# A decoder trunk on one core: the rounded weights begin at eight different byte offsets in their buffers

## The chip, the cores and the metric

The kernel runs on one core of one Trainium2 chip. The metric is the time of one execution on the device, in microseconds (us). The engines are named as in the profile: PE is the matrix engine (its matmuls) and PEld its loads of weights, which overlap the matmuls; DVE is the vector engine, ACT the scalar engine, POOL the GpSimd engine, and SP issues most of the DMAs.

## The reference

The kernel computes a trunk of two layers on 512 tokens of width 1024, in float32. Layer 0 mixes tokens with a gated delta rule, layer 1 with attention over a window of 128 tokens that reads one shared projection of keys and values. After each mixer comes a gated channel mixer with a short convolution.

```python
for layer in range(DEPTH):                       # DEPTH = 2
    if layer < N_A_LAYERS:                       # layer 0
        h = h + gated_deltanet(rmsnorm(h, a_norm_w[i]), a_w_in[i], ..., a_w_out[i])
    else:                                        # layer 1
        k_sh, v_sh = shared_kv(h, kv_norm_w, w_kv)
        h = h + sliding_window_sink_attention(rmsnorm(h, b_norm_w[j]), k_sh, v_sh, b_w_q[j], ...)
    h = h + conv_gated_mlp(rmsnorm(h, ffn_norm_w[layer]), ffn_w_up[layer], ..., ffn_w_down[layer])
return rmsnorm(h, final_norm_w)
```

Nearly all of its arithmetic is in products with weight matrices: `a_w_in` (1024 by 6176), `a_w_out` (2048 by 1024), `w_kv`, `b_w_q`, `b_w_o`, and for each layer `ffn_w_up` (1024 by 5632) and `ffn_w_down` (2816 by 1024).

## The kernel before, in words

Activations lie transposed, with features on the 128 partitions and the 512 tokens along a row, so a matmul has a 128 by 128 block of a weight matrix as its stationary operand and 512 tokens (or half of them, 256) as its moving one. To keep the accuracy of float32 at the speed of the rounded type `float32r`, every operand is split into a rounded part and the rest: `whi` and `wlo` for weights, `xh` and `xl` for activations. A product is three matmuls, `whi*xh`, `whi*xl` and `wlo*xh` (`mm3`, L165, L166, L167). In the down projections and in a part of the output projection, a scheme of seven half products in place of eight is used, with 256 tokens to a matmul (`product`, L1049, L1050, L1051); the attention's query and output projections use `one_by_one` (L1336, L1338, L1340).

A weight block comes from memory by a DMA of 1 MB into a tile `stage` (two buffers; every third one in the down projections into `st3`). Then a **casting** makes the two parts: `cast` (L131) and, for a tile filled in two pieces, `weights` with `cast_to` (L152, L155). ACT copies the block into `whi` with rounding (L135 or L158) and DVE subtracts that from the block into `wlo` (L136 or L159). Each of `whi` and `wlo` has three buffers of 4096 bytes per partition, eight blocks of 128 columns one after the other, so block `k` of a buffer begins 512 bytes after block `k-1`, and one load of weights reads 512 consecutive bytes in each partition. There are 288 castings in the program: 49 for the input projections, then those of the output projection, of layer 0's channel mixer, of the attention and of layer 1's channel mixer.

All large tiles of the kernel begin at multiples of 512 bytes; the tiles `gap_x` and `gap_w`, to which nothing is written, fill up what small constants leave. The three buffers of `whi` lie at 204288, 208384 and 212480, those of `wlo` at 216576, 220672 and 224768, and `stage` at 187904 and 196096. Constants such as `ident` and `identr` (the unit matrix, plain and rounded) lie at odd places, both at 288 bytes past a multiple of 512.

The order of the instructions in the first part comes from a table of numbers (`ORDER`), later from the order in the code with priorities, and in the attention PE's order is written out by hand.

Of the kernel before, what the change touches and what calls it, by code (L numbers as in the profile page):

```python
# [9 lines left out]
F32R = mybir.dt.float32r  # L10
# [7 lines left out]
P = 128  # L18
# [26 lines left out]
def kernel(  # L45
# [37 lines left out]
    def nm(s):  # L83
        cnt[0] += 1
        return f"{s}_{cnt[0]}"

    wpool = ctx.enter_context(tc.tile_pool(name="weights", bufs=1, side="right"))
# [41 lines left out]
        return w[r0 : r0 + kt * P, c0 : c0 + 256].rearrange("(k p) c -> p k c", p=P)  # L129

    def cast(st, kt, half, m=P):  # L131
        hi = wpool.tile([P, 8, P], F32R, tag="whi", bufs=3, name=nm("whi"))
        lo = wpool.tile([P, 8, P], F32R, tag="wlo", bufs=3, name=nm("wlo"))
        src = st[:, :kt, half * P : half * P + m]
        S.copy(hi[:, :kt, :m], src)  # L135
        V.tensor_tensor(lo[:, :kt, :m], src, hi[:, :kt, :m].bitcast(F32), op=ALU.subtract)  # L136
        return hi, lo
# [8 lines left out]
    def cast_rows(rows, half):  # L146
        w = weights()
        for i, r in enumerate(rows):
            cast_to(w, 2 * i, r[:, :, half * P : half * P + P])
        return w  # L150

    def weights():  # L152
        return [wpool.tile([P, 8, P], F32R, tag=t, bufs=3, name=nm(t)) for t in ("whi", "wlo")]

    def cast_to(w, at, src):  # L155
        n = src.shape[1]
# [135 lines left out]
    def project(c0, i):  # L292
        if c0 not in held_stage:
            held_stage[c0] = load_stage(win, 0, 8, c0)
        ps = bank("d")
        passes[c0 + P * i] = mm3(ps[:], cast(held_stage[c0], 8, i), KD, xh, xl)
        return ps
# [14 lines left out]
    S.dma_start(gst[:, :, 0:16], win[:, c_b : c_b + 16].rearrange("(k p) c -> p k c", p=P))  # L312
    S.dma_start(gst[:, :, 32:48], win[:, c_b + 16 : c_b + 32].rearrange("(k p) c -> p k c", p=P))
    gw = cast(gst, KD, 0, m=48)
    gps = bank("d")
    mm3(gps[:48, :], gw, KD, xh, xl, m=48)
# [62 lines left out]
    def hc(ap):  # L379
# [45 lines left out]
        tag="f",  # L425
# [351 lines left out]
    for pos, word in enumerate(" ".join(ORDER).split(), 1):  # L777
        name, _, later = word.partition("@")
# [117 lines left out]
    def ffn(l, h, last=False):  # L896
# [22 lines left out]
        for t0, t1 in ((0, 12), (12, NF)):  # L919
# [3 lines left out]
            for t in range(t0, t1, 2):  # L923
                if l == 0 and t == 6:
                    bias_rows()
                sg = load_stage(wup, 0, 8, t * P)
                sv = load_stage(wup, 0, 8, DFF + t * P)
                f = []
                for j in range(2):
                    a = up(cast(sg, 8, j), t + j, "ga")  # L930
                    S.activation(a[:], a[:], AF.Silu)  # L931
                    b = up(cast(sv, 8, j), NF + t + j, "va")
                    V.tensor_tensor(b[:], a[:], b[:], op=ALU.mult)  # L933
                    f.append(b)
                sevens.append(forms(*f, rows, plain))
# [122 lines left out]
    def seven_products(sts, srcs, parts, sevens, hp, odd):  # L1058
# [3 lines left out]
        for u in range(2):  # L1062
# [19 lines left out]
            yield  # L1082
        e = bank("p" if odd else "g")[:, 0:256]
        w4 = weights()
        for u in range(2):
            w = cast(sts[u], 2 * len(parts[u]), 0)
# [16 lines left out]
    def seven_products_late(sts, parts, sevens, hp):  # L1103
# [11 lines left out]
        add(h11, a)  # L1115
        add(h11, b)
        ws, w4 = [], weights()
        for u in range(2):
            ws.append(cast(sts[u], 2 * len(parts[u]), 0))
# [453 lines left out]
```

## Time and profile before

| what | value |
|---|---|
| median of 2 runs | 1395.07 us (1393.67 to 1396.46) |
| the profiled execution | 1399.02 us |
| its span, first to last instruction | 1396.9 us |
| granted PE clock over the span | 0.996 |
| instructions | 22206 |
| DMA | 154.97 MB, mean 111 GB/s |

The profile page gives each engine's busy time in the span, the chain of waits that ended last, and groups of equal instructions by line with their count and mean time. The trace behind it can be asked for one line, for a stretch of time, or for a timeline. A matmul's end in it is modelled and the next one begins before it, so the pace of PE is read from where successive matmuls begin, not from how long one lasts.

### The profile page before, as it was taken

Reading aid. Unit: us, or ns where it says so; the run is one execution under the profiler, and the core shown is the slowest. Engines: PE = TensorE matmul, PEld = TensorE weight load, DVE = VectorE, ACT = ScalarE, POOL = GpSimd, SP = SyncE. Lnnn points to the kernel's source line nnn. Section 1 sums busy time; section 2 is a strip of 40 time slices with the busy share of each in tenths; the row PEclk is TensorE's granted clock in tenths of the full one; section 3 lists DMA queues with packets and bytes.
Section 4 is the critical chain, followed back from the end, with each engine's and each line's share of the span. In section 5 each row is a group of like instructions: output and inputs, shape, how many; then the busy total and the mean of one; then the engine's idle time right before and its main releaser. Section 6 shows DMA issues by size and latency. Waiting matters only on the chain.

```text
span 1396.9 us, 22206 instructions
## 1 busy us (share of the span) xinstructions
PE 1374.1 (98%) x8520; PEld 1171.4 (84%) x8520; DVE 1142.2 (82%) x2152; ACT 765.0 (55%) x1483; POOL 15.1 (1%) x33
## 2 busy tenths in 40 slices
PE   7999999999999999999999999999999999999998
PEld 5788888878887998889988889877788889988897
DVE  5896896978867987889958899788658889878996
ACT  7765575757558455544434446677545444444443
POOL 1000000000100000000000000000000000000000
PEclk9999999999999999999999999999999999999999
DMA  5334154162567432321343224312122221432222
GB/s 162 97 100 144 46 168 142 61 197 91 172 204 241 135 132 92 120 68 66 111 151 121 74 85 135 121 59 74 61 91 91 91 94 63 145 103 81 96 76 76
DMA packets 164029, 154.97 MB, mean 111 GB/s; under 512 B 24340, under 2 KB 150869, under 8 KB 163925
## 3 DMA queue, kind: packets, MB, share of 16 engines
q1 hardware_dynamic: 161522, 153.11, 34.2%
q8 instruction: 67, 1.10, 0.3%
q10 hardware_dynamic: 2403, 0.46, 0.2%
q14 instruction: 37, 0.30, 0.1%
HBM read 136.74 MB, written 15.75 MB: 109 GB/s over the span
## 4 chain that ended last, share of the span: by engine, by line
PE 91%; DVE 3%; DMA 2%; ACT 2%; issue 1%; ACTq 0%; DVEq 0%; SPq 0%
PE d L165 20%; PE d L167 19%; PE d L166 19%; PE g L201 2%; PE d L1051 2%; PE d L1049 2%; PE d L1050 2%; PE s L1050 1%; PE s L1049 1%; PE s L1051 1%; PE d L1336 1%; PE d L1340 1%; PE d L1338 1%; PE g L1050 1%; PE g L1051 1%; PE g L1049 1%
## 5 line engine op out<-in xcount | busy, mean ns | idle before, releaser
L165 PE MATMUL d<-xh,whi 128*128 128x512 f32 x1128 | 443.9, 396 | 1.5 <-ACT whi L135 1.3
L167 PE MATMUL d<-xh,wlo 128*128 128x512 f32 x1128 | 443.3, 395 | 0.5 <-DVE wlo L136 0.5
L166 PE MATMUL d<-xl,whi 128*128 128x512 f32 x1128 | 442.3, 394 | 0.0
L135 ACT CAST whi<-stage 128x1024 fp32r<-128x1024 f32 (+2 forms) x238 | 231.5, 977 | 227.4 <-PE d L166 131.5
L136 DVE TENSOR_TENSOR wlo<-stage,whi 128x1024 fp32r<-128x1024 f32 (+2 forms) x238 | 268.6, 1131 | 54.7 <-ACT whi L135 53.0
L165 PEld LDWEIGHTS d<-xh,whi 128*128 128x128 f32 x1128 | 212.2, 188 | 46.2 <-ACT whi L135 1.8
L167 PEld LDWEIGHTS d<-xh,wlo 128*128 128x128 f32 x1128 | 212.0, 188 | 44.5 <-DVE wlo L136 1.2
L166 PEld LDWEIGHTS d<-xl,whi 128*128 128x128 f32 x1128 | 212.2, 188 | 42.9
L283 DVE SCALAR_TENSOR_TENSOR acc<-d,cwc,acc 128x511 f32<-128x511 f32 (+2 forms) x96 | 70.2, 737 | 5.6 <-ACT acc L280 4.8
L909 DVE TENSOR_TENSOR sz<-d,p6s 128x512 f32<-128x512 f32 x58 | 40.0, 689 | 39.3 <-PE d L167 37.2
L931 ACT ACTIVATE dt<-dt 128x512 f32<-128x512 f32 x44 | 27.8, 632 | 80.8 <-DVE dt L914 80.8
L914 DVE SCALAR_TENSOR_TENSOR va<-sz,fcw,va 128x511 f32<-128x511 f32 (+1 forms) x58 | 43.4, 748 | 2.1 <-ACT va L912 1.2
L914 DVE SCALAR_TENSOR_TENSOR dt<-sz,fcw,dt 128x511 f32<-128x511 f32 (+1 forms) x58 | 43.4, 747 | 1.7 <-ACT dt L912 0.9
L564 DVE TENSOR_TENSOR sT<-sT,p6s 64x31 f32<-64x31 f32 (+15 forms) x124 | 40.8, 329 | 1.6
L558 DVE TENSOR_TENSOR p6s<-sN,sT 64x31 f32<-64x31 f32 (+15 forms) x124 | 40.6, 327 | 1.5
L1405 ACT ACTIVATE dt<-dt,sm 128x256 f32<-128x256 f32 (+1 forms) x64 | 30.1, 471 | 21.5 <-DVE sm L1388 21.5
L135 ACT CAST whi<-st 128x768 fp32r<-128x768 f32 (+1 forms) x30 | 23.8, 792 | 31.3 <-PE g L1050 8.5
L909 DVE TENSOR_TENSOR zl<-d,p6s 128x512 f32<-128x512 f32 x30 | 20.7, 688 | 22.7 <-PE d L167 22.7
L693 ACT ACTIVATE rq<-o 128x128 f32<-128x128 f32 x64 | 19.0, 297 | 35.7 <-DVE o L688 26.2
L933 DVE TENSOR_TENSOR va<-dt,va 128x512 f32<-128x512 f32 x44 | 30.4, 691 | 1.2
L136 DVE TENSOR_TENSOR wlo<-st,whi 128x768 fp32r<-128x768 f32 (+1 forms) x30 | 27.0, 902 | 2.1 <-ACT whi L135 1.7
L912 ACT ACTIVATE dt<-sz,normc,fcw 128x512 f32<-128x512 f32 x29 | 23.6, 814 | 7.1 <-DVE sz L909 6.9
(865 smaller groups left out, 2973.6 us busy)
## 6 DMA issues: line engine op xcount, KB each, us to landing
stage<-in_ffn_w_up_dram SPq DMA_DIRECT2D x44, 1024.0 KB, 4.9
stage<-in_a_w_in_dram SPq DMA_DIRECT2D x23, 1024.0 KB, 5.5
stage<-in_ffn_w_down_dram SPq DMA_DIRECT2D x16, 768.0 KB, 4.9
stage<-in_a_w_out_dram SPq DMA_DIRECT2D x8, 1024.0 KB, 6.3
st<-in_ffn_w_down_dram SPq DMA_DIRECT2D x8, 768.0 KB, 5.3
zd<-sz SPq DMA_DIRECT2D x16, 256.0 KB, 2.0
od<-o SPq DMA_DIRECT2D x16, 256.0 KB, 2.4
stage<-in_b_w_q_dram SPq DMA_DIRECT2D x4, 1024.0 KB
```

Of the source, the lines that this page charges most:

```text
L135: S.copy(hi[:, :kt, :m], src)
L136: V.tensor_tensor(lo[:, :kt, :m], src, hi[:, :kt, :m].bitcast(F32), op=ALU.subtract)
L165: PE.matmul(ps, hi[:, k, :m], xh[k], start=first and k == 0, stop=False)
L166: PE.matmul(ps, hi[:, k, :m], xl[k][:], start=False, stop=False)
L167: done.append(PE.matmul(ps, lo[:, k, :m], xh[k], start=False, stop=last and k == kt - 1))
L283: V.scalar_tensor_tensor(acc[:, d:], ps[:, : T - d], col, acc[:, d:], op0=ALU.mult, op1=ALU.add)
L564: V.tensor_tensor(Tm[:, s + 1 : 32, 0:m], Tm[:, s + 1 : 32, 0:m], tv, op=ALU.subtract)
L909: V.tensor_tensor(u[:], ps[:], rs[:], op=ALU.mult)
L914: V.scalar_tensor_tensor(acc[:, d:], u[:, : T - d], tap(2 - d, t), acc[:, d:], op0=ALU.mult, op1=ALU.add)
L1049: PE.matmul(ps, w[0][:, wk, :], hi, start=first and k == 0, stop=False, **kw)
L1050: PE.matmul(ps, w[0][:, wk, :], lo, start=False, stop=False, **kw)
L1051: PE.matmul(ps, w[1][:, wk, :], hi, start=False, stop=k == n - 1, **kw)
```

## The change

`cast` now takes its two tiles from `weights`. `weights` allocates buffers of 4608 bytes in place of 4096, counts its calls, and returns a view of 4096 bytes that begins `d` elements of 4 bytes into the buffer. Up to the 84th call `d` is 0. After that it is taken from `PLACES`, each entry for fourteen calls: 16 bytes for calls 85 to 97, 256 bytes for 98 to 111, then 0, 64, 128, 192, 32, 96, 16, 256, 0, 64, 128, 192, and 32 bytes for calls 280 to 288. The 85th call is in the up projection of layer 0's channel mixer.

```diff
     def cast(st, kt, half, m=P):
-        hi = wpool.tile([P, 8, P], F32R, tag="whi", bufs=3, name=nm("whi"))
-        lo = wpool.tile([P, 8, P], F32R, tag="wlo", bufs=3, name=nm("wlo"))
+        hi, lo = weights()
         src = st[:, :kt, half * P : half * P + m]
...
+    PLACES = [0, 16, 32, 48, 8, 24, 4, 64]
+    rounded = [0]
+
     def weights():
-        return [wpool.tile([P, 8, P], F32R, tag=t, bufs=3, name=nm(t)) for t in ("whi", "wlo")]
+        flat = [wpool.tile([P, 9 * P], F32R, tag=t, bufs=3, name=nm(t)) for t in ("whi", "wlo")]
+        rounded[0] += 1
+        d = PLACES[rounded[0] // 14 % 8] if rounded[0] > 84 else 0
+        return [t[:, d : d + 8 * P].rearrange("p (k c) -> p k c", k=8) for t in flat]
```

The larger buffers move their neighbours: `whi` now lies at 201216, 205824 and 210432, `wlo` at 215040, 219648 and 224256, and `stage` at 184832 and 193024, all of them multiples of 512 still. No other tile moves. On each of the five engines the instructions, their operands' shapes, their order and their waits are the same as before, row for row; only addresses differ.

## The prediction

> **What bounds the kernel now.** I read the page's first part (how busy each engine is), then the chain of waits, and then a table by stretches of time, since only addresses change and the question is which engine could feel an address.
>
> ```profile
> PE 1374.1 (98%) x8520; PEld 1171.4 (84%) x8520; DVE 1142.2 (82%) x2152; ACT 765.0 (55%) x1483; POOL 15.1 (1%) x33
> ...
> PE 91%; DVE 3%; DMA 2%; ACT 2%; issue 1%; ACTq 0%; DVEq 0%; SPq 0%
> PE d L165 20%; PE d L167 19%; PE d L166 19%; PE g L201 2%; PE d L1051 2%; PE d L1049 2%; PE d L1050 2%; PE s L1050 1%; PE s L1049 1%; PE s L1051 1%; PE d L1336 1%; PE d L1340 1%; PE d L1338 1%; PE g L1050 1%; PE g L1051 1%; PE g L1049 1%
> ```
>
> PE is the bound: it makes up 91% of the chain, and the lines that carry it are the products with rounded weights. So the time depends on the step from one such matmul to the next. The timeline shows that step, for 512 tokens and for 256 (columns: start in us, modelled length, engine and line, operands):
>
> ```profile
> 1100.12 0.39 PE L167 MATMUL d<-xh,wlo 128*128 128x512 f32 x1
> 1100.35 0.39 PE L165 MATMUL d<-xh,whi 128*128 128x512 f32 x1
> 1100.57 0.39 PE L166 MATMUL d<-xl,whi 128*128 128x512 f32 x1
> 1100.80 0.39 PE L167 MATMUL d<-xh,wlo 128*128 128x512 f32 x1
> ...
> 1190.30 0.28 PE L1049 MATMUL s<-f,whi 128*128 128x256 f32 x1
> 1190.42 0.28 PE L1050 MATMUL s<-f,whi 128*128 128x256 f32 x1
> 1190.54 0.28 PE L1051 MATMUL s<-f,wlo 128*128 128x256 f32 x1
> ```
>
> The wide step is 0.68/3, or 0.227 us; the narrow one is 0.12 us. The stretches give the same with what else is busy. Their bounds are those of the change's groups of fourteen castings: 585 to 649 us is where calls 85 to 97 are used (16 bytes), and so on (columns: stretch, its length, then PE, PEld, DVE, ACT and POOL with busy us and count, PE clock, DMA share, GB/s):
>
> ```profile
> core 0: us, PE busy (x) PEld busy (x) DVE busy (x) ACT busy (x) POOL busy (x), PEclk, DMA share, GB/s
> 585.00:649.00 64.00, 64.00 (x296) 53.49 (x295) 54.04 (x81) 30.61 (x42) 0.00 (x0) 1.00 0.26 86
> 649.00:680.00 31.00, 30.96 (x257) 30.62 (x255) 29.70 (x54) 14.02 (x21) 0.00 (x0) 1.00 0.32 103
> ...
> 721.00:797.00 76.00, 76.00 (x337) 62.93 (x336) 62.85 (x89) 35.32 (x49) 0.00 (x0) 1.00 0.28 95
> ...
> 839.00:864.00 25.00, 25.00 (x209) 24.85 (x208) 24.48 (x48) 14.07 (x24) 0.00 (x0) 1.00 0.36 117
> ...
> 949.00:1052.00 103.00, 102.79 (x646) 82.82 (x646) 71.67 (x184) 59.16 (x138) 0.00 (x0) 1.00 0.20 66
> 1052.00:1128.00 76.00, 76.00 (x337) 62.93 (x336) 63.70 (x93) 36.85 (x51) 0.00 (x0) 1.00 0.30 97
> ...
> 1335.00:1361.00 26.00, 24.99 (x207) 24.61 (x206) 24.89 (x50) 12.02 (x21) 0.00 (x0) 1.00 0.31 102
> ```
>
> PE is busy through all of these. DVE, the next engine, has room in the wide stretches (62.85 of 76 us) and next to none in three narrow ones: 29.70 of 31, 24.48 of 25 and 24.89 of 26 us.
>
> **The change, part by part.** No instruction is added, removed or moved, no DMA, no wait. Three things read or write at new addresses: PE's loads of weights, ACT's rounding copy, DVE's subtraction.
>
> First the counts. Of 204 castings after the 84th, 28 fall on place 0 and keep their offset. Counted in the changed code, the other places carry these matmuls, wide and narrow: 16 bytes 600 and 36; 32 bytes 270 and 186; 96 bytes 336 and none; 64 bytes 528 and 108; 128 bytes 384 and 189; 192 bytes none and 420; 256 bytes 144 and 396. I part them in two: 16, 32 and 96 are no multiples of 64 (1206 wide, 222 narrow, 1428 in all), the rest are (1056 wide, 1113 narrow). Together 3597 matmuls.
>
> *Loads.* The trace of before already loads weights from other places than multiples of 512:
>
> ```profile
> L165 PEld LDWEIGHTS d<-xh,whi 128*128 128x128 f32 x1120 | 211.3, 189 | 45.4 <-ACT whi L135 1.8 <-issue 0.6 <-ACT xh L175 0.5
> L468 PEld LDWEIGHTS g<-mnegr,identr x16: 187/188/192, 51.0 to 317.9; 128*128 128x128 f32 x16
> L594 PEld LDWEIGHTS s<-Xg,nt x128: 101/108/108, 129.0 to 386.8; 32*32 32x32 f32 x128
> L602 PEld LDWEIGHTS s<-sy,pz x128: 101/108/108, 136.6 to 393.4; 32*32 32x32 f32 x128
> L1432 PEld LDWEIGHTS p<-acc,Vp x152: 132/137/137, 916.9 to 998.8; 128*64 128x64 f32 x152
> ```
>
> `identr` of L468 has the same shape and type as `whi` and begins 288 bytes past a multiple of 512, so 32 past one of 64; its load has a median of 188 ns, as L165's has a mean of 189. L602 loads from steps of 128 bytes, L594 always from 128 past: 101/108/108 ns both. L1432's `Vp` blocks begin at 0 and 256: 132 to 137 ns. The load's length thus shows no price of the place.
>
> Whether the next matmul is late is a second question, and the timeline around L468 answers it nearly:
>
> ```profile
> 50.76 0.39 PE L165 MATMUL d<-xh,whi 128*128 128x512 f32 x1
> 50.99 0.39 PE L467 MATMUL g<-gr,skr 128*128 128x512 f32 x1
> 51.22 0.40 PE L468 MATMUL g<-mnegr,identr 128*128 128x512 f32 x1
> 51.45 0.39 PE L166 MATMUL d<-xl,whi 128*128 128x512 f32 x1
> 51.68 0.40 PE L467 MATMUL g<-gr,skr 128*128 128x512 f32 x1
> 51.92 0.39 PE L468 MATMUL g<-mnegr,identr 128*128 128x512 f32 x1
> 52.15 0.40 PE L167 MATMUL d<-xh,wlo 128*128 128x512 f32 x1
> 52.38 0.39 PE L165 MATMUL d<-xh,whi 128*128 128x512 f32 x1
> 52.61 0.40 PE L166 MATMUL d<-xl,whi 128*128 128x512 f32 x1
> 52.85 0.50 PE L467 MATMUL g<-gr,skr 128*128 128x512 f32 x1
> ```
>
> From 50.76 to 52.85 are nine steps in 2.09 us, 232 ns each, 5 over the plain 227. But L167 to L165 to L166 here, with buffers at multiples of 512, take 230 each as well, so the 5 ns belong to this busy place and not to `identr`. As the upper end I still charge 5 ns to every matmul off a multiple of 64: 1428 by 5 is 7.1 us. The lower end is nothing, unless the present step holds a cost that a new place removes; that is a rival below. I take 1 us, close to nothing, because the row nearest in kind, L468's load, shows no difference at the trace's step of 1 ns.
>
> By the Trainium skill ("SBUF — State Buffer", Specifications) the buffer memory has lines of 16 bytes, with a price for each new line. All eight places are multiples of 16, so by that rule a load would touch 32 lines wherever it begins and the sum would be 0; were the line 64 bytes, places 16, 32 and 96 would touch nine lines in place of eight. No run so far shows the line.
>
> *Castings.* Here too before has unaligned neighbours:
>
> ```profile
> L914 DVE SCALAR_TENSOR_TENSOR dt<-sz,fcw,dt 128x511 f32<-128x511 f32 x29 | 21.6, 746 | 0.9 <-ACT dt L912 0.9
> L176 DVE SCALAR_TENSOR_TENSOR xl<-h,normc,xh 128x512 fp32r<-128x512 f32 x16 | 11.3, 749 | 0.0
> L220 ACT CAST identr<-ident x1: 281/281/281, 8.8 to 8.8; 128x128 fp32r<-128x128 f32 x1
> L135 ACT CAST whi<-stage 128x1024 fp32r<-128x1024 f32 x174 | 181.8, 1050 | 156.1 <-PE d L166 117.0 <-DMA stage<-in_ffn_w_up_dram 11.0 <-PE d L1338 7.9
> L135 ACT CAST whi<-stage 128x512 fp32r<-128x512 f32 x17 | 10.4, 618 | 13.9 <-PE p L1050 4.4 <-DMA stage<-in_ffn_w_down_dram 3.3 <-DVE wlo L136 3.2
> L136 DVE TENSOR_TENSOR wlo<-stage,whi 128x1024 fp32r<-128x1024 f32 x174 | 212.1, 1221 | 50.4 <-ACT whi L135 49.1 <-ACT rt L869 0.7 <-PE s L662 0.2
> ```
>
> L914 reads and writes `dt` from 4 bytes in: 746 ns, against 749 for L176 that begins at multiples of 512 with one element more. ACT's copy into `identr`, 288 past, took 281 ns for 128 columns; from the two rows of L135, 432 ns for 512 columns, a copy of 128 at a multiple of 512 would take 618 - 384 x 0.844, or 294. So neither is slower off its place. Were they, most of it would be hidden: ACT idles 156.1 us ahead of L135 because the buffer is not free yet, and DVE has 13 us of room in 76. Only the three tight stretches have none. How long DVE works there on instructions that read `whi` or write `wlo`, the stretches' sum for that tile tells:
>
> ```profile
> sum 82.00, DVE 36.37; mean DVE 12.12
> ```
>
> 25% on these 36.37 us, far over what L914 allows, would be 9.1 us, less the 2.9 us of room in those stretches (1.3 + 0.52 + 1.11): 6 us as the upper end, and 0 as the value taken, from L914.
>
> *Base addresses.* The buffers move by multiples of 512. Before, the eight blocks of each buffer already begin at eight successive multiples of 512, and the step is 227 or 120 ns through all of them (rows above). Nothing is charged. `stage` moves by 3072 bytes and its DMAs keep their shape: nothing.
>
> The sum is +1 us against the profiled execution of 1399.02 us, which is 0.3% over the median of 1395.07. Against the median it gives 1396.
>
> **The rivals.**
>
> *Slower: a load that begins off a multiple of 64 is no longer hidden under a matmul.* For it: the load lasts 188 ns of a step of 227, so 39 ns more would show, and in the narrow steps loads overlap each other already. If it lasted half as long again, 94 ns, a wide step would become 282 ns, 55 more by 1206, and a narrow one up to 94 more by 222: 66 + 21 = 87 us, or 1482. It passes 2% (27.9 us) from 19.5 ns per matmul on these 1428; if every place but 0 paid, from 7.8 ns on 3597. Against it: L468's load at 188 ns. Its weak side is that no row begins at 16 past, where 636 of the matmuls are.
>
> *Slower: DVE becomes the bound.* To lose 27.9 us in the three tight stretches alone, their 36.37 us of subtractions would have to grow by 85%, to cover 27.9 and the room of 2.9. L914 speaks against any such growth.
>
> *Faster: the step itself holds a conflict.* Wide minus narrow is 107 ns for 256 columns, so 512 columns take 214 and 13 ns per matmul are something else. If these came of operands that begin alike, and new places removed them, 3597 by 13 is 46.8 us: 1348. Against it: the step is the same for eight blocks at different addresses, and L468 with both operands elsewhere is no faster. The Trainium skill ("TensorE: Matmul & The Clock Gate", Back-to-back issue gap) gives N/2.4 + 2.5 ns, 216 for 512 columns, an estimate that leaves 11 ns of this step open and would give some 40 us to such a conflict, about 1355; the trace does not agree with that pace here, and nothing in it says that the place is why.
>
> *The change doesn't reach what its words say.* It starts at the 85th casting, at 585 us, well after the output projection. That shortens what it can touch to the last 803 us, and is in the counts above.
>
> **How the numbers follow.** No difference to speak of: 0.81. Loads that stick out, or DVE: 0.14 for over 2% (0.10 and 0.04). A conflict removed: 0.05 for over 2%. Two per cent is about what a measurement of this kernel can tell from no change. The likeliest time is 1396. The range takes the upper ends of loads and castings, 7.1 + 6, on 1395, and a milder form of the first rival (another 5 ns per matmul, 7.1): 1415. Downward, a sixth of the conflict's 46.8 us: 1387.
>
> **What would show it.** Two stretches have equal work, fourteen castings and 336 wide matmuls: one at place 64 (721 to 797 us before), one at place 16 (1052 to 1128). They should again take 76 us each. Loads of `whi` should stay at 188 ns, L135 at 1050 and L136 at 1221 ns for 1024 columns. If the second stretch is longer than the first, the place of the load or of the casting counts, and the timeline's step (227 or more) says which. A step under 227 in the groups off 0 would make the third rival right; DVE near 100% where it had 82% the second.

## The result, and the profile after

| | before | after |
|---|---|---|
| median, us | 1395.07 (1393.67 to 1396.46, 2 runs) | 1404.34 (1403.34 to 1405.33, 2 runs) |
| ratio to before, 95% interval | | 1.0059 (1.0042 to 1.0076) |
| span of the profiled execution, us | 1396.9 | 1403.2 |

The changed kernel is 0.6% slower: inside the range, clear of noise, and nine times the 1 us that the sum gave. Its profile page shows the same picture as before, PE as the bound:

```profile
PE 1379.5 (98%) x8520; PEld 1168.8 (83%) x8520; DVE 1142.8 (81%) x2152; ACT 764.4 (54%) x1483; POOL 15.1 (1%) x33
...
PE 90%; DVE 3%; DMA 3%; ACT 2%; issue 1%; SPq 0%; DVEq 0%; ACTq 0%
```

DVE and ACT are busy as long as before (1142.2 and 765.0 us then); PE is busy 5.4 us longer for the same 8520 matmuls. The stretches by group of fourteen castings show where. The columns are those of the same view of before; the rows are, in order, place 16 for the first time, place 64, place 16 for the second time, place 256 with wide matmuls, and a narrow stretch at place 0 and, for some of its matmuls, 256:

```profile
585.00:644.00 59.00, 59.00 (x262) 48.87 (x261) 49.70 (x73) 26.62 (x36) 0.00 (x0) 1.00 0.25 82
718.10:796.50 78.40, 78.40 (x337) 63.26 (x337) 63.01 (x89) 35.58 (x48) 0.00 (x0) 1.00 0.26 87
...
1054.60:1133.00 78.40, 78.40 (x337) 63.54 (x336) 65.21 (x94) 37.07 (x51) 0.00 (x0) 1.00 0.30 96
1133.10:1165.00 31.90, 31.90 (x142) 26.41 (x141) 27.23 (x41) 13.95 (x20) 0.00 (x0) 1.00 0.23 77
1180.00:1211.00 31.00, 31.00 (x260) 31.00 (x260) 28.47 (x50) 12.30 (x17) 0.00 (x0) 1.00 0.48 157
```

The two stretches of equal work, 76 us each before, both take 78.4 now, with the same 337 matmuls, while DVE has over 13 us of room. The timeline inside the stretch at place 64 gives the step (L170 to L172 are L165 to L167 of before), and the rows after the dots are narrow ones at place 64:

```profile
749.64 0.39 PE L170 MATMUL d<-xh,whi 128*128 128x512 f32 x1
749.87 0.40 PE L171 MATMUL d<-xl,whi 128*128 128x512 f32 x1
750.11 0.39 PE L172 MATMUL d<-xh,wlo 128*128 128x512 f32 x1
750.34 0.40 PE L170 MATMUL d<-xh,whi 128*128 128x512 f32 x1
...
1213.91 0.28 PE L1054 MATMUL s<-qT,whi 128*128 128x256 f32 x1
1214.03 0.28 PE L1055 MATMUL s<-qT,whi 128*128 128x256 f32 x1
1214.14 0.28 PE L1056 MATMUL s<-qT,wlo 128*128 128x256 f32 x1
1214.26 0.28 PE L1054 MATMUL s<-sy,whi 128*128 128x256 f32 x1
1214.38 0.28 PE L1055 MATMUL s<-sy,whi 128*128 128x256 f32 x1
1214.49 0.28 PE L1056 MATMUL s<-sy,wlo 128*128 128x256 f32 x1
1214.61 0.28 PE L1054 MATMUL d<-vt,whi 128*128 128x256 f32 x1
```

A wide step is 0.70/3, 0.233 us, where it was 0.227; a narrow one 0.70/6, 0.117, where it was 0.120. So the wide steps became longer and the narrow ones shorter at this place. Over the whole trace, the means of all steps from one matmul with rounded weights to the next (those over 300 ns, which hold waits, left out; "first" and "second" are the two groups of castings at place 16):

| place, bytes | 0 | 16, first | 16, second | 32 | 64 | 96 | 128 | 192 | 256 |
|---|---|---|---|---|---|---|---|---|---|
| wide step, ns | 228 | 226.7 | 233.3 | 233 | 233.3 | 234 | 232.4 | none | 226.8 |
| matmuls | 1452 | 264 | 336 | 242 | 528 | 310 | 384 | | 144 |

The 228 of place 0 is a mean over two things. In an unbroken stretch the step there is 226.7 ns; but the first steps after other work on PE, up to ten of them, take some 231 ns, and the early part of the program is full of such breaks.

What did not change are the lengths of the castings and of the loads beside the wide matmuls, in the groups by line (L134 and L135 cast, L170 loads):

```profile
L134 ACT CAST whi<-stage 128x1024 fp32r<-128x1024 f32 x174 | 181.5, 1048 | 162.8 <-PE d L171 119.6 <-DMA stage<-in_ffn_w_up_dram 10.6 <-PE d L1343 8.3
L135 DVE TENSOR_TENSOR wlo<-stage,whi 128x1024 fp32r<-128x1024 f32 x174 | 212.0, 1221 | 47.1 <-ACT whi L134 43.5 <-DMA Xg<-td 2.2 <-ACT rt L874 0.7
L170 PEld LDWEIGHTS d<-xh,whi 128*128 128x128 f32 x1120 | 210.8, 188 | 47.2 <-ACT whi L134 1.4 <-ACT xh L180 0.7 <-issue 0.6
```

### The profile page after: what moved, and what is told of

Read it like the earlier page. It is cut to its first block, busy times and chain, and to the rows that moved or that the text cites. A ratio compares the mean times of both kernels' runs of the same rounds, so it can differ in the third digit from the quotient of the medians.

```text
span 1403.2 us, 22206 instructions
## 1 busy us (share of the span) xinstructions
PE 1379.5 (98%) x8520; PEld 1168.8 (83%) x8520; DVE 1142.8 (81%) x2152; ACT 764.4 (54%) x1483; POOL 15.1 (1%) x33
## 4 chain that ended last, share of the span: by engine, by line
PE 90%; DVE 3%; DMA 3%; ACT 2%; issue 1%; SPq 0%; DVEq 0%; ACTq 0%
PE d L170 19%; PE d L172 19%; PE d L171 19%; PE d L1056 2%; PE d L1054 2%; PE g L206 2%; PE d L1055 2%; PE s L1055 1%; PE s L1054 1%; PE s L1056 1%; PE d L1341 1%; PE d L1345 1%; PE d L1343 1%; PE g L1056 1%; PE g L1055 1%; PE g L1054 1%
## 5 line engine op out<-in xcount | busy, mean ns | idle before, releaser
L170 PE MATMUL d<-xh,whi 128*128 128x512 f32 x1128 | 445.8, 397 | 1.4 <-ACT whi L134 0.9
L172 PE MATMUL d<-xh,wlo 128*128 128x512 f32 x1128 | 445.2, 396 | 0.5 <-DVE wlo L135 0.5
L134 ACT CAST whi<-stage 128x1024 fp32r<-128x1024 f32 (+2 forms) x238 | 231.2, 975 | 234.3 <-PE d L171 134.8
L135 DVE TENSOR_TENSOR wlo<-stage,whi 128x1024 fp32r<-128x1024 f32 (+2 forms) x238 | 268.2, 1129 | 51.1 <-ACT whi L134 47.2
L170 PEld LDWEIGHTS d<-xh,whi 128*128 128x128 f32 x1128 | 211.8, 188 | 48.0 <-ACT whi L134 1.4
L172 PEld LDWEIGHTS d<-xh,wlo 128*128 128x128 f32 x1128 | 212.2, 188 | 47.0 <-DVE wlo L135 1.2
L134 ACT CAST whi<-st 128x768 fp32r<-128x768 f32 (+1 forms) x30 | 23.8, 792 | 31.7 <-PE g L1055 7.9
L135 DVE TENSOR_TENSOR wlo<-st,whi 128x768 fp32r<-128x768 f32 (+1 forms) x30 | 26.9, 900 | 1.8 <-ACT whi L134 1.4
```

Source lines behind the costliest of these rows:

```text
L170: PE.matmul(ps, hi[:, k, :m], xh[k], start=first and k == 0, stop=False)
L172: done.append(PE.matmul(ps, lo[:, k, :m], xh[k], start=False, stop=last and k == kt - 1))
```

## The experiments

The first question was whether the place does it at all, or the moved buffers. Theory P: the place in the buffer sets PE's step. The ratios below are against the kernel before, run on the same chip.

**All castings at place 0, with the larger buffers.**

```diff
-        d = PLACES[rounded[0] // 14 % 8] if rounded[0] > 84 else 0
+        d = 0
```

> The larger buffers and the moved base addresses stay, but every casting begins at place 0. Theory P (the place within 512 bytes sets the step of the matmuls): steps of 227 and 120 ns throughout, time as before, 1395 us. Rival B (the moved bases of whi, wlo and stage cost the time): about 1404 us, and slower somewhere at place 0.

Measured: 1395.45 us, ratio 0.9995 (0.9985 to 1.0006); mean steps 227.6 and 120.7 ns, against 227.6 and 120.6 before. The larger buffers and the new base addresses cost nothing that shows.

**All castings at place 64.** The line becomes `d = 16` (16 elements of 4 bytes).

> Every casting, the first 84 too, begins 64 bytes in. Theory P: all 3990 wide matmuls step at 233.3 ns instead of 226.7, +26 us, and all 2139 narrow ones at 118 instead of 120, -4 to -5 us: about 1417 us. Rival T (the longer steps belong to the later part of the program, not to the place): the first 585 us stay as they were, about 1404 us or less.

Measured: 1413.20 us, ratio 1.0120 (1.0104 to 1.0137). Every wide stretch, the first one from 13.8 us on too, steps at 233.4 ns in the mean; the narrow step has a mean of 116.6. The place does it, anywhere in the program. The gain in the narrow steps was larger than expected in ns: they take one of two paces, 117.8 ns in some stretches and 113.3 in others.

**All castings at place 192,** the one that no wide matmul of the changed kernel had: `d = 48`.

> Every casting begins 192 bytes in; no wide matmul of the changed kernel had this place. Theory F (every place that is no multiple of 256 makes the wide step 233 ns): about 1413 us, like place 64. Rival Q (each place has a step of its own, whole slots of 6.7 ns beside the 213.3 ns of 512 columns; at 192 the wide step may be 220 or 227): 227 ns would give about 1394 us, 220 ns about 1370 us. Narrow steps 118 ns by both.

Measured: 1398.96 us, ratio 1.0019 (1.0008 to 1.0030); steps 229.3 and 118.4 ns. Neither was quite right: the place has a step of its own, as rival Q says, but in the mean over 227. In most unbroken stretches 226, 229 and 232 ns take turns, 228.9 in the mean; from 105 to 125 us it is 233.3, at the same place.

The next question was what the place is counted from. All moving operands (`xh`, `xl` and the tiles of the seven products) lay at multiples of 512, so the place of the weights could count by itself (theory A), or its distance to the moving operand (theory R). Two kernels move the constants, the activations and `stage` by 64 bytes, by 16 more elements in `gap_x` and 16 fewer in `gap_w`; the weights begin at multiples of 512 in the first and 64 bytes past them in the second.

**Moving operands at 64, weights at 0.** (The buffers begin at 64, so `d` is 448 bytes.)

```diff
-    cp.tile([P, 40], F32, name="gap_x")
+    cp.tile([P, 56], F32, name="gap_x")
...
-        d = PLACES[rounded[0] // 14 % 8] if rounded[0] > 84 else 0
+        d = 112
...
-    wpool.tile([P, 120], F32, tag="gap", bufs=1, name="gap_w")
+    wpool.tile([P, 104], F32, tag="gap", bufs=1, name="gap_w")
```

> All tiles of activations and stage begin 64 bytes past multiples of 512, the weights at multiples of 512. Theory A (the place of the weights alone counts): wide 227, narrow 120 ns, 1395 us. Theory R (the place of the weights counted from that of the moving operand, here 64 bytes behind it): as at place 192, narrow 118 ns, and not 227 with 120.

**Moving operands at 64, weights at 64.** As above, with `d = 0`.

> All tiles of activations, stage and the weights begin 64 bytes past multiples of 512. Theory A (the place of the weights alone counts): wide 233 and narrow 113 to 118 ns as in the kernel with every casting at 64, about 1413 us. Theory R (only the distance of the two counts, here 0): wide 227, narrow 120 ns, 1395 us.

The same stretch of layer 1's up projection, in four kernels: all at place 64, then weights at 64 with the moving operands at 64 too, then all at place 192, then weights at 0 with moving operands at 64 (the PE column, busy us and count, is the one to read):

```profile
1050.00:1140.00 90.00, 90.00 (x387) 72.12 (x387) 72.90 (x104) 42.83 (x59) 0.00 (x0) 1.00 0.27 88
```

```profile
1050.00:1140.00 90.00, 90.00 (x399) 74.55 (x398) 74.69 (x107) 41.87 (x58) 0.00 (x0) 1.00 0.29 94
```

```profile
1050.00:1140.00 90.00, 90.00 (x395) 73.84 (x394) 73.20 (x105) 42.28 (x58) 0.00 (x0) 1.00 0.29 94
```

```profile
1050.00:1140.00 90.00, 90.00 (x395) 73.86 (x394) 74.83 (x108) 42.75 (x58) 0.00 (x0) 1.00 0.29 94
```

With weights at 64, 387 matmuls fit into 90 us; with the moving operands put at 64 as well, 399 do, as many as in the kernel with everything at place 0. And weights 64 behind give the 395 of place 192. The mean steps over the whole trace agree to 0.3 ns: 227.6 and 120.6 for equal places at 64 (before: 227.6 and 120.6), 229.3 and 118.1 for weights 64 behind (place 192: 229.3 and 118.4). Theory A falls, and theory R holds for the means: what counts is the distance between the two operands, and 256 bytes bring it round, since place 256 steps like 0 and 64 behind like 192 ahead. But the distance alone doesn't settle the pace of a stretch. From 1010 to 1030 us place 192 and weights 64 behind part, at equal distances: the one steps at 228.9 ns, the other at 233.3 (first place 192, then weights at 0 with moving operands at 64):

```profile
1010.00:1030.00 20.00, 20.00 (x89) 16.40 (x88) 11.93 (x16) 8.46 (x12) 0.00 (x0) 1.00 0.16 52
```

```profile
1010.00:1030.00 20.00, 20.00 (x87) 16.19 (x87) 13.68 (x19) 8.80 (x12) 0.00 (x0) 1.00 0.31 103
```

Nor do these kernels tell which pair it is: the weights and the moving operand of the same matmul, or the moving operand of one and the weights that are loaded meanwhile for the next. Within each of them the two distances are the same.

The times are 1398.39 us with the weights at 64, ratio 1.0009 (0.9998 to 1.0020), and 1401.73 us with the weights at 0, ratio 1.0038 (1.0026 to 1.0051). The second is 2.8 us over place 192. In the two profiled executions most of this difference has arisen by 444 us, in layer 0's mixer, and not in steps between matmuls with rounded weights; its cause is open.

**`whi` at 64, `wlo` at 0.** Does each load pay, or does a whole stretch take one pace?

```diff
-        d = PLACES[rounded[0] // 14 % 8] if rounded[0] > 84 else 0
-        return [t[:, d : d + 8 * P].rearrange("p (k c) -> p k c", k=8) for t in flat]
+        return [t[:, d : d + 8 * P].rearrange("p (k c) -> p k c", k=8) for t, d in zip(flat, (16, 0))]
```

> whi begins 64 bytes in, wlo at place 0; two loads in three are of whi. Theory L (each load at an odd place delays the matmul beside it): of three wide steps two are 233 ns and one 227 or the other way round, mean 231, about +17 us. Rival M (a whole stretch takes one pace): all three 233, +26 us of wide steps, or all three 227, no difference.

Measured: 1411.35 us, ratio 1.0103 (1.0069 to 1.0137). Over the whole trace the steps are 230.1 ns from `whi` to the same `whi`, 233.3 on to `wlo`, 233.0 from `wlo` to the next `whi`, 232.1 overall. These means mix two kinds of stretch, with the same places in both: layer 0's up projection steps at 231.1 ns, with 226, 236 and 232 taking turns, and layer 1's at 233.3, where each of the three has a mean of 231 or more. The rows are of these two, in the windows in which the kernel before had 337 matmuls each:

```profile
721.00:797.00 76.00, 76.00 (x331) 61.74 (x330) 61.37 (x89) 34.95 (x48) 0.00 (x0) 1.00 0.30 98
1052.00:1128.00 76.00, 76.00 (x327) 61.06 (x326) 61.42 (x88) 35.55 (x48) 0.00 (x0) 1.00 0.25 83
```

So layer 0's stretch has the mean of theory L and layer 1's that of theory M. That steps within a triple differ decides nothing, since at place 192 they differ too, with one distance for all three. How the loads share the price stays open.

Then there was place 16, at 227 ns in one stretch and 233 in another, with the same addresses in both. Theory S: the pace that comes in is carried on.

**All castings at place 16:** `d = 4`.

> Every casting begins 16 bytes in, the place that stepped at 227 ns in one stretch of the changed kernel and at 233 ns in another. Theory S (at place 16 the pace of the matmuls before is carried on): which pace it takes at the start decides, 1391 us if 227 ns, and both paces may appear in the run. Rival W (place 16 is like 64 and the stretch at 585 us is the exception): 233 ns nearly everywhere, about 1417 us.

Measured: 1410.64 us, ratio 1.0098 (1.0080 to 1.0115). Both paces are in the run. Layer 0's up projection steps at 233.3 ns in the mean, with 522 matmuls of all kinds in 120 us (533 with everything at place 0), layer 1's at 226.7, with 399 in 90 us (as many as at place 0):

```profile
520.00:640.00 120.00, 120.00 (x522) 97.01 (x521) 96.17 (x140) 57.38 (x79) 0.00 (x0) 1.00 0.29 95
1050.00:1140.00 90.00, 90.00 (x399) 74.53 (x398) 74.19 (x107) 43.49 (x59) 0.00 (x0) 1.00 0.29 96
```

In the unbroken stretches of both up projections the pace stays the same from end to end; after a down projection's narrow matmuls it can be another. That doesn't show that the pace is carried on from the matmuls before. The next run puts that to the test.

**One casting before the stretch at 64.** Only the 84th casting differs from the changed kernel; the weights of the stretch itself keep their addresses.

```diff
         d = PLACES[rounded[0] // 14 % 8] if rounded[0] > 84 else 0
+        d = 16 if rounded[0] == 84 else d
```

> The changed kernel with one difference: the 84th casting, whose 24 wide matmuls come right before those of calls 85 to 95 at place 16, begins 64 bytes in. Theory S (at place 16 the wide matmuls carry on at the pace that they come with): the 264 wide matmuls of calls 85 to 95, 226.7 ns in the changed kernel, step at 233 ns, so some 60 us take 1.8 us more. Rival E (something else in that stretch keeps it at 227): 24 steps of 233 ns and then 227 ns as before.

Measured, one execution of each: 1406.47 us, beside 1392.49 for the kernel before. The stretch that follows, in the changed kernel and then in this one:

```profile
586.00:644.00 58.00, 58.00 (x257) 48.06 (x256) 48.70 (x72) 25.79 (x35) 0.00 (x0) 1.00 0.25 82
```

```profile
586.00:644.00 58.00, 58.00 (x250) 46.95 (x250) 48.48 (x71) 26.14 (x35) 0.00 (x0) 1.00 0.26 84
```

257 matmuls before, 250 now. All 264 wide steps of the eleven castings after the 84th went from 226.7 to 233.3 ns, up to 60 us after the only thing that differs had passed. The wide-only kernel below, whose 84th casting is at place 0 again, has 226.7 ns in this stretch, like the changed kernel, so chance from one execution to the next doesn't explain it. Theory S is shown for this place: at 16 bytes either pace lasts, and the one that comes in right before is kept.

**What the loss is made of.** Two kernels split the change: the odd places, that is all but 0, go to the castings of wide matmuls alone, or to those of the seven half products alone. `narrow` is true in the calls from `seven_products` and `seven_products_late`.

```diff
-        d = PLACES[rounded[0] // 14 % 8] if rounded[0] > 84 else 0
+        d = PLACES[rounded[0] // 14 % 8] if rounded[0] > 84 and not narrow else 0
```

> The changed kernel, but castings of the seven half products stay at place 0; only wide matmuls get the odd places. If the loss is the sum of the wide steps: 336 + 336 + 192 wide ones by 6.7 ns, 336 and 288 by 5.8, 96 by 5.8 and 240 by 4.5 make 11 us, so 1406 us, a little above the changed kernel. If castings or narrow steps have a part in the loss: below 1404 us.

For the other one, `and narrow`.

> The changed kernel, but only castings of the seven half products get the odd places; wide ones stay at place 0. If the loss is the sum of the wide steps: none of it is left, and the narrow steps (118 ns at places other than 0 and 256) give 1 to 2 us: 1393 to 1395 us. If castings at odd places cost time in the narrow stretches, where DVE is nearly full: over 1397 us.

Measured: wide only 1405.78 us, ratio 1.0073 (1.0060 to 1.0087); narrow only 1393.72 us, ratio 0.9999 (0.9990 to 1.0009). The loss is in the wide steps. By the table of steps, less 226.7 (in the attention, where other matmuls come between, less the 228.5 ns of before), 11.1 us: 2.2 for place 64 at 718 us, 0.6 and 1.6 for the two of 128, 1.1 for 32, 1.9 for 96, 2.2 for the second 16, 1.3 for the second 64, 0.2 at the end. Measured: 10.6 us between the medians. The changed kernel's 9 lies within the noise of that, so what the narrow steps gave back there isn't shown.

**The shorter narrow step put to use.** Castings of the seven half products at 192, then at 64, all others at place 0. Each of their calls gets a `d` that `cast` hands on to `weights`; one of them:

```diff
-            w = cast(sts[u], 2 * nk, 0)
+            w = cast(sts[u], 2 * nk, 0, d=48)
```

> Castings for the seven half products (256 tokens) begin 192 bytes in, all others at place 0. Theory P: wide steps 227, narrow steps 118 ns, 2079 narrow matmuls by 2 ns, about -4 us: 1391 us, below both kernels. Rival D (the narrow stretches are set by DVE, so a shorter step there only makes PE wait): no difference, 1395 us.

> Castings for the seven half products begin 64 bytes in, all others at place 0. If PE sets the pace of the narrow stretches, the shorter step (113 to 118 ns against 118 at place 192) saves up to 2 to 7 us more than place 192 did there: 1386 to 1391 us. Rival D (DVE, which is busy 94 to 98% there, sets it): about as with place 192, 2 to 5 us below the kernel before.

Measured: 1394.80 us, ratio 0.9985 (0.9976 to 0.9995), and 1392.60 us, ratio 0.9982 (0.9974 to 0.9991). Both beat both kernels, by little, and place 64 brought nothing more over 192 that can be told from the times. Two things take the gain. One is the pace: at place 64 it is 117.8 ns, as at 192, all through layer 0's down projection, and 113.3 in much of layer 1's. The rows show a piece of each, with everything at place 0, then at 192, then at 64:

```profile
646.00:704.00 58.00, 57.64 (x478) 57.27 (x477) 52.81 (x93) 24.06 (x34) 0.00 (x0) 1.00 0.33 108
1160.00:1217.00 57.00, 56.96 (x474) 56.75 (x474) 52.26 (x92) 24.54 (x35) 0.00 (x0) 1.00 0.35 111
```

```profile
646.00:704.00 58.00, 57.80 (x489) 57.53 (x489) 53.90 (x95) 24.63 (x35) 0.00 (x0) 1.00 0.35 111
1160.00:1217.00 57.00, 56.80 (x481) 56.53 (x480) 52.81 (x93) 25.22 (x36) 0.00 (x0) 1.00 0.36 117
```

```profile
646.00:704.00 58.00, 57.48 (x483) 56.85 (x483) 53.06 (x94) 24.29 (x35) 0.00 (x0) 1.00 0.32 104
1160.00:1217.00 57.00, 56.80 (x489) 56.27 (x488) 52.97 (x93) 26.05 (x36) 0.00 (x0) 1.00 0.31 103
```

The other is waiting, as rival D said. In the profiled execution with place 64 the shorter pace is worth 8 us over all narrow steps, but waits, read as what steps over 135 ns have in excess, grow by 4 us against place 0, so about half of the gain is left; at 192 it is 4.5 us, less 1.4. In the chain of waits of the kernel with place 64 DVE has 5%, up from 3% before, and the subtraction of a casting appears in it:

```profile
PE 87%; DVE 5%; ACT 3%; DMA 3%; issue 1%; DVEq 0%; ACTq 0%; SPq 0%
PE d L169 19%; PE d L171 19%; PE d L170 19%; PE g L205 2%; PE d L1055 2%; DVE wlo L135 2%; PE d L1053 1%; PE d L1054 1%; PE d L1340 1%; PE d L1344 1%; PE d L1342 1%; PE s L1053 1%; PE s L1055 1%; PE s L1054 1%; PE p L1436 1%
```

## Why the prediction was right or wrong

- **The bound: right.** In the wide stretches the time follows PE's step; ACT and DVE did the same work at the same lengths. In the narrow ones it follows the step by about half.
- **Castings and base addresses: right.** L134 has 1048 ns for 1050, L135 1221 for 1221; the moved buffers alone gave a ratio of 0.9995, and odd places for the narrow castings, where DVE has no room, 0.9999.
- **Loads: the mis-sized term.** It was charged 1 us of at most 7.1, and is about 11 us in the wide steps: 11.1 by the table, 10.6 measured with the wide places alone. The step that failed is the choice of the nearest row. It took the load's length, 188 ns at `identr`, but that length stays at 188 and the matmul's step grows all the same. The longer steps around L468, 232 ns, were laid to the busy place, and that reading holds as far as the trace goes: soon after, nine steps between matmuls with rounded weights, all at distance 0, take 2.08 us, 231 ns each.

  ```profile
  54.46 0.40 PE L166 MATMUL d<-xl,whi 128*128 128x512 f32 x1
  54.70 0.40 PE L167 MATMUL d<-xh,wlo 128*128 128x512 f32 x1
  54.93 0.39 PE L165 MATMUL d<-xh,whi 128*128 128x512 f32 x1
  55.16 0.39 PE L166 MATMUL d<-xl,whi 128*128 128x512 f32 x1
  55.39 0.40 PE L165 MATMUL d<-xh,whi 128*128 128x512 f32 x1
  55.62 0.39 PE L166 MATMUL d<-xl,whi 128*128 128x512 f32 x1
  55.85 0.40 PE L167 MATMUL d<-xh,wlo 128*128 128x512 f32 x1
  56.08 0.39 PE L165 MATMUL d<-xh,whi 128*128 128x512 f32 x1
  56.31 0.39 PE L166 MATMUL d<-xl,whi 128*128 128x512 f32 x1
  56.54 0.39 PE L167 MATMUL d<-xh,wlo 128*128 128x512 f32 x1
  ```

  So the rows around L468, whose two operands lie 128 bytes apart, could neither show a price of a few ns nor exclude one, and they were no ground for charging almost nothing.
- **The range: in part luck.** The loads alone went past their upper end. The time stayed under 1415 because the castings, allowed 6 us, cost nothing, and because another 7.1 us had been added for a milder first rival. And 2% was too coarse a bound for what can be told from no change: this 0.6% is clear of an interval of 0.2% to either side.
- **The wrong set.** The price was put on places off a multiple of 64. Places 64 and 128 pay as well, 256 doesn't, and 16 pays or not. The narrow matmuls, charged like the wide ones, gain 1 to 2 ns a step at all places but 256.
- **The line of 16 bytes.** That every place is a multiple of it was true and did not help. The Trainium skill's rule ("SBUF — State Buffer", Specifications) says nothing of the distance between two operands, by which the step goes here.
- **The slower rival** had the right sign and the right engine but another mechanism: no load sticks out, its price is 6.7 ns and not the 19.5 that would pass 2%, and so the time stays within 2%.
- **The faster rival** is half right: in the narrow steps there was something to gain, 2 to 7 ns of the 13 that the step has over its columns. They gain at distances at which the wide steps lose, and waits take about half of it. What was held against this rival, eight blocks with the same step, was no test, since all eight lie at multiples of 512.
- **What would show it** half worked: the 76 us of the two stretches of equal work failed, at 78.4 us, and the timeline's step said why. Their comparison said nothing, as both grew alike.

## What to carry to other kernels

Where PE is the bound with one load per matmul, read its step from where successive matmuls begin, and keep weights and moving operand at the same offset modulo 256 bytes for 512 columns; here that was worth up to 6.7 ns of 233, and other distances shortened the step only at 256 columns. A question of addresses is asked of pairs of operands, since neither address alone predicted a step. And a price of a few ns can't be read in a corner of the trace where the steps vary by as much for another reason: it takes a row from an unbroken stretch, or a run that changes the one thing.

## What the runs showed of the hardware that was not expected

- The step of a matmul with `float32r` operands depends on the distance of its two operands modulo 256 bytes. In the mean over the trace it is with 512 columns 227.6 ns at 0, 233.4 at 64, 232.4 at 128 (in the attention and around it only), 229.3 at 192; with 256 columns 120.6 at 0, 116.6 at 64, 118.4 at 192. The wide paces of 226.7 and 233.3 ns are 6.7 ns apart, and so are the narrow ones of 120 and 113.3; why by this amount was not tried.
- At distances other than 0 more than one pace can last through a stretch: at 16 bytes 226.7 and 233.3 ns, at 192 228.9 and 233.3, and with 256 columns at 64 and 192 117.8 and 113.3. At 16, 24 matmuls ahead of a stretch decided which it took for the next 264; for the other distances it was not tried what decides. Unbroken stretches at distance 0 had one pace in every trace here, 226.7 and 120.0 ns, after up to ten slower wide steps at their start.
- The Trainium skill ("TensorE: Matmul & The Clock Gate", Step-by-step: what each phase is for) gives PE two separate read ports, so that loading the next weights takes nothing from the running matmul's reads. The runs fit badly with that: the pace goes by where the two lie to each other, 226.7 ns at distance 0 and 233.3 at 64, with the load's own length unchanged at 188 ns beside wide matmuls. That the two reads meet somewhere is argued from this, not shown; which of them waits, and for what, stays open.
